# Elementwise sums and products of GpSimd moved to VectorE in a two-block, fp32-accurate network on one core

## The chip, the core and the metric

One core of a Trainium2 chip runs the whole network in one launch. TensorE (PE in the profile) does matmuls into PSUM, VectorE (DVE) and ScalarE (ACT) do elementwise work, GpSimd (POOL) does elementwise work on SBUF alone, and SyncE (SP) issues DMAs. The metric is the device time of one execution in microseconds; the shown time is the median of three runs.

## The reference, cut to what matters

A sequence of 512 tokens of width 1024 goes through two blocks. The first has an even layer (linear recurrent unit and a gated convolution) and an odd one (spatial gating and forgetting attention), each followed by a convolutional gated feed-forward layer. The second, with 256 context tokens beside the 512, has two layers of three branches:

```
h = rms_norm(x, g) * (1 + scale) + shift
aq, ak, av, az, bq, ..., cz, gm = split_proj(h @ w_in)      # a: differential attention, b: mLSTM, c: neighbourhood
...
proj = einsum('btnw,nwd->btnd', stack(ys), w_br)            # three branches
y = sum(sigmoid(gm) * proj, axis=2) @ w_out
x = x + gate * y
```

All inputs and outputs are float32 and the products have to be nearly as exact as that.

## The kernel before, in words

Activations lie with their channels on the 128 partitions and tokens along the free dimension. A matmul operand is held as a high and a low part, both in a form that PE multiplies in one pass (`H` and `L` for the layer's input, `wh` and `wl` for a weight), and each product is three matmuls, high by high, high by low and low by high (`mm3`). A weight is loaded raw (`ws`), ACT copies it to `wh`, DVE subtracts to get `wl` (`wload`). Queries and keys are stacked the same way into halves of 64 rows (`stack`).

The gate projections `gm` of block 2 save matmuls by a scheme of seven half-size products instead of eight. Its left operands are sums of the halves of a pair of weights, which `wpair` forms in place with four 128x512 sums (`ws` and `w2`, on GpSimd; 24 pairs in all). Its right operands are sums of halves of the layer's input, which `halves` forms at the start of each layer: it first adds `H` and `L` back together (eight sums per layer, on GpSimd) and then does four more sums for each group and splits them (DVE and ACT).

Other work that GpSimd has: sums of squares for the norms (`Stream.square`, most of them), a product in `even`, masks on weights and on rows (`odd`, `scan`), products with per-head factors (`mixed`, `head_out`), the rotary sum (`branch_a.prep`), the sum of two directions and one product in `scan`, a product with the norm in `out_proj`, and fills.

The order is not that of the code. `Order` (lines 200 to 440) records every operation with a cost (`_cost`), the tiles it touches and its dependencies, and `flush` then issues them one at a time: on each engine the earliest-recorded operation that can start soonest by the costs, as long as a buffer is free. So each engine runs a fixed list in order, and a change of an operation's engine or cost may reorder all five lists behind it. The costs of the two forms in question are

```
        if eng == "pool":
            return 146 + (2.1 if op == "tensor_tensor" else 3.3) * size
...
        two = not psum and n_in <= 1 and op in ("tensor_copy", "tensor_scalar", "memset")
        return 95 + size / (1.92 if two else 0.96)
```

The planner has no term for two engines that hinder each other. All recorded operations carry one line, 486, in the profile, so groups are told apart by tile names: `s` and `t` are the working buffers of block 2 and block 1, `P` a PSUM bank, `tn` a small one, `C` the constants. A DVE operation that the compiler makes for a reduction with two inputs is named CUSTOM_DVE_ANT_0, or ISA in the order.

Of the kernel before, what the change touches and what calls it, by code (L numbers as in the profile page):

```python
# [9 lines left out]
F32 = mybir.dt.float32  # L10
# [3 lines left out]
ALU = mybir.AluOpType  # L14
# [4 lines left out]
T = 512  # L19
# [491 lines left out]
class Kern:  # L511
# [68 lines left out]
    def wpair(self, srcs):  # L580


        nc = self.nc
        self.n_ += 1
        raw = []
        for i, src in enumerate(srcs):
            st = nc.tile(self.wp, [128, 1088], F32, "wst", self.WST, f"ws{self.n_}_{i}")
            nc.sync.dma_start(out=st[:, :1024], in_=src.rearrange("p k m -> p (k m)"))
            raw.append(st)
        s2 = nc.tile(self.wp, [128, 512], F32, "w2", 1, f"w2{self.n_}")  # L590
        a11, a12, a21, a22 = (raw[i][:, 512 * j:512 * j + 512] for i in range(2) for j in range(2))
        out = {}

        def put(x, names, tags=("whi", "wlo", 1088, 4)):
            self.n_ += 1
            n = 512 * len(names)
            hi = nc.tile(self.wp, [128, tags[2]], F32R, tags[0], tags[3], f"wh{self.n_}")[:, :n]
            lo = nc.tile(self.wp, [128, tags[2]], F32R, tags[1], tags[3], f"wl{self.n_}")[:, :n]
            self.split(hi, lo, x[:, :n])
            for i, a in enumerate(names):  # L600
                out[a] = [y[:, 512 * i:512 * i + 512].rearrange("p (k m) -> p k m", k=4) for y in (hi, lo)]

        sub = lambda o, x, y: nc.gpsimd.tensor_tensor(o, x, y, op=ALU.subtract)
        put(raw[0], ("a11", "a12"))
        sub(a11, a11, a21)
        sub(s2, a22, a11)
        put(s2, ("s2",), ("w2h", "w2l", 512, 1))
        sub(a12, a12, s2)
        put(raw[0], ("s3", "s4"))
        nc.gpsimd.tensor_tensor(a21, a21, a22, op=ALU.add)  # L610
        put(raw[1], ("s1", "a22"))
        return out

# [73 lines left out]
class Stream:  # L687
# [7 lines left out]
    def square(self, x):  # L695
        K, nc = self.K, self.K.nc
        sq = self.new()[:, :self.n]
        nc.scalar.activation(sq, x, AF.Square)
        if self.acc is not None:
            e = nc.vector if self.k in VADD else nc.gpsimd  # L700
            e.tensor_tensor(sq, sq, self.acc, op=ALU.add)
        self.k += 1
        self.acc = sq

# [31 lines left out]
def block1(K, X, out, dbg, mods, B, es):  # L736
# [101 lines left out]
    def even(pre):  # L838
# [29 lines left out]
        for j in range(4):  # L868
            nc.scalar.activation(hh[j], hh[j], AF.Sqrt, scale=0.25)
        for j in range(4):  # L870
            nc.gpsimd.tensor_tensor(ix[j], ix[j], hh[j], op=ALU.mult)
            nc.vector.tensor_tensor_scan(hh[j], aa[j], ix[j], 0.0, ALU.mult, ALU.add)
        for j in range(0, 4, 2):
            for j, p in zip((j, j + 1), scaled(proj(W[4 + j], W[5 + j]), R)):
# [18 lines left out]
    def odd():  # L893
# [23 lines left out]
        wt = [t3(), t3()]  # L917
        for i in range(2):
            nc.sync.dma_start(out=wt[i], in_=A["sgu_wt"][:, 4 * i:4 * i + 4])
            nc.gpsimd.tensor_tensor(wt[i], wt[i], K.c("keep").unsqueeze(1).to_broadcast([128, 4, 128]),  # L920
                                    op=ALU.mult)
        bb = t3()
        nc.sync.dma_start(out=bb, in_=A["sgu_bb"])
# [16 lines left out]
        def mixed():  # L940
# [8 lines left out]
            rg = K.rsqrt(sv, 32)  # L949
            nc.vector.tensor_scalar(sv, rg, 0.5, None, op0=ALU.mult)  # L950
            for n in range(4):
                nc.gpsimd.tensor_tensor(hc(gt[n]), hc(gt[n]),
                                        sv[:, n * 8:(n + 1) * 8].unsqueeze(2).to_broadcast([128, 8, 64]), op=ALU.mult)
            yield
            for j in range(4):
# [18 lines left out]
        def prep(j):  # L974
# [23 lines left out]
            for hp in range(2):  # L998
                st.append(K.stack(q_, k_, hp, t2, T, T))
                h = 2 * j + hp  # L1000
                cb.append(t2())
                nc.sync.dma_start(out=cb[hp], in_=cd[h:h + 1, :].partition_broadcast(128))
                cm.append(t3())
                nc.gpsimd.tensor_tensor(cm[hp], cb[hp].rearrange("p (a b) -> p a b", a=4),
                                        K.c("cmask").unsqueeze(1).to_broadcast([128, 4, 128]), op=ALU.add)
            heads[j] = vt, st, cb, cm
            yield
# [164 lines left out]
SQUARES = 11000.0  # L1172
RATES = 32000.0
COND = 60000.0
VADD = (6, 7)
FIRST = 7

GM = (0, 0, 0, 1, 1, 1, 1, 2, 2, 2, 1, 1)
# [2 lines left out]
class Block2:  # L1181
# [95 lines left out]
    def halves(self, n):  # L1277

        K, nc = self.K, self.nc
        b = self.tk = {q: [] for q in ("b11", "b21", "b22", "t1", "t2", "t3", "t4")}  # L1280
        for k in range(4):
            for nm, r, c in (("b11", k, 0), ("b21", k + 4, 0), ("b22", k + 4, n)):
                b[nm].append((K.H[:, r, c:c + n], K.L[:, r, c:c + n]))
        self.tn = n
        for k in range(4):
            x, y = self.s(2 * n), self.s(2 * n)
            for a, r in ((x, k), (y, k + 4)):
                nc.gpsimd.tensor_tensor(a, K.H[:, r, :2 * n].bitcast(F32), K.L[:, r, :2 * n].bitcast(F32), op=ALU.add)
            b11, b12, b21, b22 = x[:, :n], x[:, n:], y[:, :n], y[:, n:]
            nc.vector.tensor_tensor(b11, b12, b11, op=ALU.subtract)  # L1290
            nc.vector.tensor_tensor(b12, b22, b12, op=ALU.subtract)
            nc.vector.tensor_tensor(b22, b22, b11, op=ALU.subtract)
            nc.vector.tensor_tensor(b21, b21, b22, op=ALU.subtract)
            for a, names in ((x, ("t1", "t3")), (y, ("t4", "t2"))):
                h, l = self.ysplit(a, 2 * n)
                for i, nm in enumerate(names):
                    b[nm].append((h[:, i * n:i * n + n], l[:, i * n:i * n + n]))
            yield
# [94 lines left out]
    def head_out(self, o, ntile, g, gate, c):  # L1393
# [7 lines left out]
        nc.vector.tensor_reduce(ss, b3(sq), axis=AX.X, op=ALU.add)  # L1401
        nc.vector.tensor_scalar(v, ss, 1.0 / 128 / c ** 2, EPS / c ** 2, op0=ALU.mult, op1=ALU.add)
        r = K.rsqrt(v, ntile)
        nc.gpsimd.tensor_tensor(b3(o), b3(o), r.unsqueeze(2).to_broadcast([128, ntile, 128]), op=ALU.mult)
        for q, b, m in self.transposes(o, [i * 128 for i in range(ntile)]):
            d = gate[:, b:b + m]
            nc.vector.scalar_tensor_tensor(d, q, g, d, op0=ALU.mult, op1=ALU.mult)
# [3 lines left out]
    def branch_a(self, lat, ctx, full, out):  # L1411
# [28 lines left out]
        def prep(h):  # L1440
# [4 lines left out]
            for nm, c in (("aq", cq), ("ak", ctx)):  # L1445
# [1 line left out]
                d, w = self.s(), self.s(T)  # L1447
                nc.vector.stream_shuffle(out=w, in_=p[0][0], mask=swap)
                nc.vector.tensor_tensor(d[:, :T], p[0][0], rc, op=ALU.mult)
                nc.gpsimd.tensor_tensor(w, w, rs, op=ALU.mult)  # L1450
                nc.gpsimd.tensor_tensor(d[:, :T], d[:, :T], w, op=ALU.add)
                self.copy(d, p[1:])
                qk.append(d)
                yield
# [133 lines left out]
    def branch_b(self, lat, ctx, full, out):  # L1588
# [31 lines left out]
        def scan(h):  # L1620
# [15 lines left out]
            for d in range(2):  # L1636
# [2 lines left out]
                nc.sync.dma_start(out=b6(m), in_=src.partition_broadcast(128))  # L1639
                nc.vector.tensor_tensor(b6(m), b6(m), cols(self.MIN, d, ntile).to_broadcast([128, ntile, 128]), op=ALU.max)  # L1640
                W = self.s(n)
                nc.gpsimd.tensor_tensor(b6(W), b6(m), K.c("maskf" if d == 0 else "maskb").unsqueeze(1)
                                        .to_broadcast([128, ntile, 128]), op=ALU.add)
                for i in range(ntile):
                    r = slice(i * 128, (i + 1) * 128)
# [5 lines left out]
                    nc.vector.tensor_tensor(W[:, b:b + e], W[:, b:b + e], p, op=ALU.mult)  # L1651

                for b, e in ((0, n),) if not full else ((0, T), (T + 128, n)) if d == 0 else ((0, n - 128),):
                    (nc.vector if d == 0 else nc.gpsimd).tensor_tensor(m[:, b:e], m[:, b:e], q[:, b:e], op=ALU.mult)
                Ws.append(W)
                qa.append(m)
                yield
# [35 lines left out]
            for d in range(2):  # L1693
                for a in range(2):
                    i = slice(a * pb, (a + 1) * pb)
                    nc.vector.tensor_tensor(b6(o[d])[:, i], O[d][a][:, :, :128],
                                            d3(da, d)[:, i].unsqueeze(2).to_broadcast([128, pb, 128]), op=ALU.mult)
            nc.gpsimd.tensor_tensor(o[0], o[0], o[1], op=ALU.add)
            z = self.silu2(self.unit("bz", h, lat, cq))
            yield  # L1700
            t = self.s(n)
# [142 lines left out]
    def out_proj(self, full, out):  # L1844
# [23 lines left out]
        for m in range(8):  # L1868
# [2 lines left out]
            nc.sync.dma_start(out=t[:, :T], in_=self.xd[:, m])  # L1871
            a = (m, w, t, lat, 0, T, S, X, 0)
            if full:
                nc.gpsimd.tensor_tensor(t[:, :T], t[:, :T], R1, op=ALU.mult)
                nc.sync.dma_start(out=t[:, T:], in_=self.A["xc"][:, m])
                if m < 5:
                    some(*a)
# [122 lines left out]
```

## Time and profile before

| | |
|---|---|
| median of 3 runs | 2883.07 us (2879.26 to 2884.18) |
| the profiled execution, its time | 2883.25 us |
| its span | 2881.5 us |
| PE, PEld (weight loads) | 98%, 85% of the span busy |
| DVE, ACT, POOL | 71%, 45%, 14% busy |
| mean granted clock of PE | 0.993 of full speed |
| matmuls | 16280 |

The span is what lies between the first and the last instruction; 1.75 us lie around it. Matmuls overlap: each is shown from its start to its end while the next has already begun, so a busy PE says little, and the waits have to be read from places where PE stood still. Block 1 fills the first 1130 us, the first layer of block 2 the next 990, the second layer the rest.

### The profile page before, as it was taken

The page shows a single profiled execution, that of the slowest core. Times are in us where ns is not written, and L with a number is a line of the kernel's source. Part 1 is how long each engine was busy: PE and PEld are TensorE (multiplying, and loading weights), DVE is VectorE, ACT ScalarE, POOL GpSimd, SP SyncE. Part 2 cuts the span into 40 slices and gives each one's busy share as a digit, 9 for nine tenths or more (in the row PEclk, how much of TensorE's full clock was granted, in tenths as well). Part 3 has the DMA queues.
Part 4 walks back from the last instruction along what each step waited for, and adds up shares of the span by engine and source line. Part 5 has one row for each costly group of instructions (what it writes and reads, how often), then busy time and mean ns, then how long its engine had stood idle before and what let it go on. Part 6 is the DMA issues. An engine that isn't in the chain of part 4 may idle for free. (4 is left out here: it accounts for less than half of the span.)

```text
span 2881.5 us, 42542 instructions
## 1 busy us (share of the span) xinstructions
PE 2831.4 (98%) x16280; PEld 2452.8 (85%) x16280; DVE 2057.3 (71%) x4049; ACT 1306.7 (45%) x2449; POOL 393.4 (14%) x285
## 2 busy tenths in 40 slices
PE   9999999999999999999999999999999999999998
PEld 7888888887888888889899989998878889989887
DVE  7878687478875875855777676575586677787765
ACT  6344234465442443754545453341256554554433
POOL 1010000010100003100211131120210121232201
PEclk9999999999999999999999999999999999999999
DMA  4333433332324423111112132254312222232362
GB/s 171 125 120 124 144 133 110 105 106 80 137 99 145 142 89 118 63 67 57 72 67 71 59 104 92 76 165 164 135 63 94 71 81 71 71 107 96 107 211 92
DMA packets 113245, 302.63 MB, mean 105 GB/s; under 512 B 11657, under 2 KB 25353, under 8 KB 113041
## 3 DMA queue, kind: packets, MB, share of 16 engines
q1 hardware_dynamic: 112896, 299.91, 30.7%
q8 instruction: 128, 2.10, 0.3%
q14 instruction: 77, 0.62, 0.1%
q10 hardware_dynamic: 144, 0.00, 0.0%
HBM read 272.26 MB, written 27.61 MB: 104 GB/s over the span
## 5 line engine op out<-in xcount | busy, mean ns | idle before, releaser
L486 PE MATMUL P<-H,wl 128*128 128x512 f32 (+2 forms) x2648 | 960.9, 363 | 4.0 <-DVE wl L486 4.0
L486 PE MATMUL P<-L,wh 128*128 128x512 f32 (+2 forms) x2648 | 961.2, 363 | 2.5 <-DVE L L486 2.5
L486 PE MATMUL P<-H,wh 128*128 128x512 f32 (+2 forms) x2648 | 960.9, 364 | 1.4 <-ACT H L486 1.4
L486 ACT ACTIVATE wh<-ws 128x1024 fp32r<-128x1024 f32 (+3 forms) x450 | 436.1, 972 | 764.3 <-PE P L486 649.1
L486 DVE TENSOR_TENSOR wl<-ws,wh 128x1024 fp32r<-128x1024 f32 (+3 forms) x450 | 523.3, 1164 | 204.3 <-ACT wh L486 202.4
L486 PEld LDWEIGHTS P<-H,wl 128*128 128x128 f32 x2648 | 500.3, 189 | 82.7 <-DVE wl L486 5.4
L486 PEld LDWEIGHTS P<-L,wh 128*128 128x128 f32 x2648 | 499.6, 189 | 83.3 <-DVE L L486 4.6
L486 PEld LDWEIGHTS P<-H,wh 128*128 128x128 f32 x2648 | 499.0, 188 | 81.4 <-ACT H L486 2.4
L486 PE MATMUL P<-s,wh 128*128 128x256 f32 (+2 forms) x1344 | 330.6, 333 | 0.0
L486 PE MATMUL P<-t,wh 128*128 128x512 f32 x960 | 301.5, 395 | 0.3 <-ACT t L486 0.3
L486 ACT ACTIVATE s<-P 128x512 f32<-128x512 f32 (+3 forms) x416 | 186.6, 482 | 222.9 <-PE P L486 202.7
L486 PE MATMUL P<-s,s 128*128 128x128 f32 (+4 forms) x1576 | 239.1, 293 | 11.9 <-DVE s L486 11.8
L486 PEld LDWEIGHTS P<-s,wh 128*128 128x128 f32 x1344 | 229.6, 189 | 17.6
L486 PEld LDWEIGHTS P<-s,s 128*128 128x128 f32 (+1 forms) x1576 | 212.8, 192 | 28.7 <-issue 10.2
L486 PE MATMUL P<-s,wl 128*128 128x256 f32 (+2 forms) x672 | 222.8, 332 | 2.1 <-DVE wl L486 2.1
L486 PEld LDWEIGHTS P<-t,wh 128*128 128x128 f32 x960 | 180.4, 188 | 43.0 <-ACT t L486 0.6
L486 ACT ACTIVATE s<-s 128x768 f32<-128x768 f32 (+7 forms) x226 | 153.3, 694 | 114.7 <-DVE s L486 97.9
L486 DVE TENSOR_TENSOR s<-s,s 128x512 f32<-128x512 f32 (+8 forms) x200 | 173.9, 875 | 26.2 <-ACT s L486 11.9
L486 PE MATMUL P<-t,wl 128*128 128x512 f32 x480 | 189.8, 395 | 0.0
L486 POOL TENSOR_TENSOR s<-s,s 128x512 f32<-128x512 f32 (+2 forms) x76 | 102.8, 1356 | 582.2 <-DVE s L486 317.7
L486 ACT ACTIVATE s<-P,tn 128x512 f32<-128x512 f32 (+1 forms) x224 | 117.8, 534 | 107.0 <-DVE tn L486 106.9
L486 ACT ACTIVATE t<-t 128x512 f32<-128x512 f32 (+4 forms) x162 | 97.5, 611 | 123.5 <-DVE t L486 122.6
(145 smaller groups left out, 3579.8 us busy)
## 6 DMA issues: line engine op xcount, KB each, us to landing
ws<-in_w2in SPq DMA_DIRECT2D x136, 512.0 KB, 3.3
ws<-in_up SPq DMA_DIRECT2D x88, 512.0 KB, 3.2
wm<-in_w_mod SPq DMA_DIRECT2D x48, 512.0 KB, 4.4
ws<-in_down SPq DMA_DIRECT2D x32, 384.0 KB, 3.1
ws<-in_w2br SPq DMA_DIRECT2D x48, 256.0 KB, 2.7
ws<-in_down SPq DMA_DIRECT2D x32, 320.0 KB, 2.9
ws<-in_w0in SPq DMA_DIRECT2D x18, 512.0 KB, 3.7
gd<-s SPq DMA_DIRECT2D x24, 384.0 KB, 2.9
```

What stands on the lines that cost most here:

```text
L486: o["f"](*o["a"], **o["k"])
```

## The change

Every sum and product that was on GpSimd is put on VectorE, 273 operations; GpSimd keeps its 12 fills. In `square` the list of steps that were already on DVE (`VADD`) goes. Nothing else is edited, but the planner now prices these operations as DVE's and orders all engines anew.

```diff
@@ wpair
-        sub = lambda o, x, y: nc.gpsimd.tensor_tensor(o, x, y, op=ALU.subtract)
+        sub = lambda o, x, y: nc.vector.tensor_tensor(o, x, y, op=ALU.subtract)
...
-        nc.gpsimd.tensor_tensor(a21, a21, a22, op=ALU.add)
+        nc.vector.tensor_tensor(a21, a21, a22, op=ALU.add)
@@ Stream.square
-            e = nc.vector if self.k in VADD else nc.gpsimd
-            e.tensor_tensor(sq, sq, self.acc, op=ALU.add)
+            nc.vector.tensor_tensor(sq, sq, self.acc, op=ALU.add)
@@ halves
-                nc.gpsimd.tensor_tensor(a, K.H[:, r, :2 * n].bitcast(F32), K.L[:, r, :2 * n].bitcast(F32), op=ALU.add)
+                nc.vector.tensor_tensor(a, K.H[:, r, :2 * n].bitcast(F32), K.L[:, r, :2 * n].bitcast(F32), op=ALU.add)
@@ head_out
-        nc.gpsimd.tensor_tensor(b3(o), b3(o), r.unsqueeze(2).to_broadcast([128, ntile, 128]), op=ALU.mult)
+        nc.vector.tensor_tensor(b3(o), b3(o), r.unsqueeze(2).to_broadcast([128, ntile, 128]), op=ALU.mult)
@@ branch_a.prep
-                nc.gpsimd.tensor_tensor(w, w, rs, op=ALU.mult)
-                nc.gpsimd.tensor_tensor(d[:, :T], d[:, :T], w, op=ALU.add)
+                nc.vector.tensor_tensor(w, w, rs, op=ALU.mult)
+                nc.vector.tensor_tensor(d[:, :T], d[:, :T], w, op=ALU.add)
...
```

The same exchange of `gpsimd` for `vector` is made in `even`, `odd`, `mixed`, `branch_b.scan` (mask, product, sum) and `out_proj`.

What it does to the order is shown at three places. The first is DVE's list at the start of block 2, where `halves` begins (`s_9695`, `s_9696`, `s_9732` are the first of its sums; `s_9672` is the first subtraction of a `stack` that PE needs next; `wl` are weights):

```order
 L486 SCALAR_TENSOR_TENSOR L<-t_2040,mod_79,H 128x512
+L486 TENSOR_TENSOR s_9695<-H,L 128x768
 L486 TENSOR_TENSOR wl_2064<-ws_2062,wh_2063 128x1024
 L486 TENSOR_TENSOR wl_2067<-ws_2065,wh_2066 128x1024
-L486 TENSOR_TENSOR wl_9799<-ws_9797,wh_9798 128x1024
+L486 TENSOR_TENSOR s_9696<-H,L 128x768
 L486 TENSOR_TENSOR s_9695<-s_9695 128x384
 L486 TENSOR_TENSOR s_9695<-s_9696,s_9695 128x384
+L486 TENSOR_TENSOR s_9696<-s_9696,s_9695 128x384
+L486 TENSOR_TENSOR s_9732<-H,L 128x768
 L486 TENSOR_TENSOR s_9672<-s_9667,s_9672 64x768
```

Three of the eight sums now stand on DVE ahead of the stack, with one more step of 128x384, and a weight's low part has gone behind it.

The second is DVE's list at the first weight pair of layer 0, inside the neighbourhood attention (`s_9973` and `s_9976` are rows of probabilities that PE transposes next, `ws_0_10056`, `ws_1_10057` and `w_10058` the pair and its sums):

```order
 L486 TENSOR_SCALAR s_9961<-s_9961,tn_9956 128x512
 L486 TENSOR_TENSOR tn_9971<-tn_9969 128x2
+L486 TENSOR_TENSOR ws_0_10056<-ws_0_10056,ws_1_10057 128x512
 L486 RECIPROCAL tn_9971<-tn_9971 128x2
+L486 TENSOR_TENSOR ws_1_10057<-ws_1_10057 128x512
 L486 TENSOR_SCALAR s_9973<-s_9973,tn_9971 128x512
 L486 TENSOR_SCALAR s_9976<-s_9976,tn_9971 128x512
+L486 TENSOR_TENSOR w_10058<-ws_1_10057,ws_0_10056 128x512
+L486 TENSOR_TENSOR ws_0_10056<-ws_0_10056,w_10058 128x512
+L486 TENSOR_TENSOR wl_10062<-w_10058,wh_10061 128x512
```

Two of the pair's four sums stand ahead of the second two rows, two behind them.

The third is PE's list in layer 1 where a head's output (`s_12235`, scaled by GpSimd before, by DVE now) is transposed into `P_12334`, between matmuls of the gates of branch b:

```order
 L486 MATMUL P_12383<-wh_12378,H 128x272
-L486 MATMUL P_12334<-C,s_12235 128x128 x4
 L486 MATMUL P_12383<-wh_12378,L 128x272
 L486 MATMUL P_12383<-wl_12379,H 128x272
@@ -12411,4 +12409,5 @@
 L486 MATMUL P_12384<-wh_12378,H 128x272
 L486 MATMUL P_12384<-wh_12378,L 128x272
+L486 MATMUL P_12334<-C,s_12235 128x128 x4
```

The transposes have gone behind 22 more matmuls.

## Rows read from the trace of the kernel before

**Rows 1.** The page, part 1: busy time, share of the span, instructions of each engine.

```profile
PE 2831.4 (98%) x16280; PEld 2452.8 (85%) x16280; DVE 2057.3 (71%) x4049; ACT 1306.7 (45%) x2449; POOL 393.4 (14%) x285
```

**Rows 2.** Timeline at 8 us: start, length, engine, line, operation, tiles, shapes, count.

```profile
8.15 0.40 PE L486 MATMUL P<-L,wh 128*128 128x512 f32 x1
8.15 0.19 PEld L486 LDWEIGHTS P<-H,wl 128*128 128x128 f32 x1
8.39 0.39 PE L486 MATMUL P<-H,wl 128*128 128x512 f32 x1
```

**Rows 3.** What PE waited for, whole span: us in total, times, longest.

```profile
PE P L486 <- DVE s L486: 21.2, 20, 4.1
PE P L486 <- DVE wl L486: 6.8, 7, 1.9
PE P L486 <- DVE t L486: 3.7, 3, 1.5
...
PE P L486 <- POOL s L486: 2.0, 2, 1.2
```

**Rows 4.** Groups by shape: count, busy us, mean ns of one, idle before.

```profile
L486 POOL TENSOR_TENSOR s<-s,s 128x512 f32<-128x512 f32 x53 | 73.6, 1389 | 388.7 <-DVE s L486 243.3 <-PE P L486 69.6 <-ACT s L486 62.2
L486 POOL TENSOR_TENSOR s<-H,L 128x768 f32<-128x768 f32 x8 | 18.1, 2294 | 34.1 <-DVE L L486 34.1
L486 DVE TENSOR_TENSOR t<-t,t 128x512 f32<-128x512 f32 x64 | 44.1, 689 | 2.5 <-ACT t L486 1.5
L486 DVE TENSOR_TENSOR s<-s,s 128x512 f32<-128x512 f32 x42 | 36.6, 874 | 2.3 <-DMA s<-cmd 2.0
L486 DVE TENSOR_TENSOR s<-s,s 128x768 fp32r<-128x768 f32 x20 | 18.9, 953 | 0.6 <-issue 0.5
```

**Rows 5.** Timeline of layer 0's `halves`, 1142 to 1172 us; GpSimd, DVE, PE.

```profile
1142.09 18.09 POOL L486 TENSOR_TENSOR s<-H,L 128x768 f32<-128x768 f32 x8 [34.13 <-DVE L L486]
...
1151.32 2.91 DVE L486 TENSOR_TENSOR wl<-ws,wh 128x1024 fp32r<-128x1024 f32 x1 [1.72 <-ACT wh L486]
...
1154.15 2.21 DVE L486 TENSOR_TENSOR s<-s 128x384 f32<-128x384 f32 x1
...
1156.47 5.51 DVE L486 TENSOR_TENSOR s<-s,s 128x384 f32<-128x384 f32 x3
...
1162.71 0.55 PE L486 MATMUL P<-s,s 128*128 128x256 f32 x1 [4.07 <-DVE s L486]
...
1171.47 0.55 DVE L486 TENSOR_TENSOR s<-s 128x384 f32<-128x384 f32 x1
```

**Rows 6.** What PE waited for, layer 1's `halves`, 2118 to 2156 us.

```profile
PE P L486 <- DVE s L486: 3.0, 1, 3.0
PE P L486 <- DVE L L486: 2.2, 2, 1.5
```

**Rows 7.** Timeline at a weight pair, 1273 to 1279 us, and one row without GpSimd.

```profile
1174.41 0.88 DVE L486 TENSOR_SCALAR s<-s,tn 128x512 f32<-128x512 f32 x2
...
1273.96 1.41 POOL L486 TENSOR_TENSOR ws<-ws,ws 128x512 f32<-128x512 f32 x1 [113.78 <-DVE wl L486]
...
1277.05 2.65 DVE L486 TENSOR_SCALAR s<-s,tn 128x512 f32<-128x512 f32 x2
...
1278.44 0.63 PE L486 MATMUL P<-C,s 128*128 128x128 f32 x4 [1.78 <-DVE s L486]
```

**Rows 8.** Timeline at a head's output in layer 1.

```profile
2479.58 1.04 POOL L486 TENSOR_TENSOR s<-s,tn 128x512 f32<-128x512 f32 x1 [8.11 <-issue]
...
2480.68 0.55 PE L486 MATMUL P<-C,s 128*128 128x128 f32 x3 [0.81 <-POOL s L486]
```

**Rows 9.** Stretches: length, PE busy (count), granted clock, DMA share, GB/s.

```profile
1161.00:1168.00 7.00, 5.29 (x25) 0.51 0.00 0
...
2154.30:2157.80 3.50, 3.50 (x18) 0.51 0.02 5
```

**Rows 10.** A slice of layer 1, all engines: length, busy (count) each, clock, DMA.

```profile
2521.00:2593.00 72.00, 68.00 (x443) 61.53 (x442) 57.53 (x138) 37.62 (x81) 22.20 (x17) 0.95 0.32 105
```

More of the change, by code (lines that the diff above doesn't have):

```diff
@@ L870, in even @@
         for j in range(4):
-            nc.gpsimd.tensor_tensor(ix[j], ix[j], hh[j], op=ALU.mult)
+            nc.vector.tensor_tensor(ix[j], ix[j], hh[j], op=ALU.mult)
             nc.vector.tensor_tensor_scan(hh[j], aa[j], ix[j], 0.0, ALU.mult, ALU.add)
@@ L919, in odd @@
             nc.sync.dma_start(out=wt[i], in_=A["sgu_wt"][:, 4 * i:4 * i + 4])
-            nc.gpsimd.tensor_tensor(wt[i], wt[i], K.c("keep").unsqueeze(1).to_broadcast([128, 4, 128]),
+            nc.vector.tensor_tensor(wt[i], wt[i], K.c("keep").unsqueeze(1).to_broadcast([128, 4, 128]),
                                     op=ALU.mult)
@@ L951, in mixed @@
             for n in range(4):
-                nc.gpsimd.tensor_tensor(hc(gt[n]), hc(gt[n]),
+                nc.vector.tensor_tensor(hc(gt[n]), hc(gt[n]),
                                         sv[:, n * 8:(n + 1) * 8].unsqueeze(2).to_broadcast([128, 8, 64]), op=ALU.mult)
@@ L1003, in prep @@
                 cm.append(t3())
-                nc.gpsimd.tensor_tensor(cm[hp], cb[hp].rearrange("p (a b) -> p a b", a=4),
+                nc.vector.tensor_tensor(cm[hp], cb[hp].rearrange("p (a b) -> p a b", a=4),
                                         K.c("cmask").unsqueeze(1).to_broadcast([128, 4, 128]), op=ALU.add)
@@ L1174 @@
 COND = 60000.0
-VADD = (6, 7)
 FIRST = 7
@@ L1641, in scan @@
                 W = self.s(n)
-                nc.gpsimd.tensor_tensor(b6(W), b6(m), K.c("maskf" if d == 0 else "maskb").unsqueeze(1)
+                nc.vector.tensor_tensor(b6(W), b6(m), K.c("maskf" if d == 0 else "maskb").unsqueeze(1)
                                         .to_broadcast([128, ntile, 128]), op=ALU.add)
@@ L1653, in scan @@
                 for b, e in ((0, n),) if not full else ((0, T), (T + 128, n)) if d == 0 else ((0, n - 128),):
-                    (nc.vector if d == 0 else nc.gpsimd).tensor_tensor(m[:, b:e], m[:, b:e], q[:, b:e], op=ALU.mult)
+                    nc.vector.tensor_tensor(m[:, b:e], m[:, b:e], q[:, b:e], op=ALU.mult)
                 Ws.append(W)
@@ L1697, in scan @@
                                             d3(da, d)[:, i].unsqueeze(2).to_broadcast([128, pb, 128]), op=ALU.mult)
-            nc.gpsimd.tensor_tensor(o[0], o[0], o[1], op=ALU.add)
+            nc.vector.tensor_tensor(o[0], o[0], o[1], op=ALU.add)
             z = self.silu2(self.unit("bz", h, lat, cq))
@@ L1873, in out_proj @@
             if full:
-                nc.gpsimd.tensor_tensor(t[:, :T], t[:, :T], R1, op=ALU.mult)
+                nc.vector.tensor_tensor(t[:, :T], t[:, :T], R1, op=ALU.mult)
                 nc.sync.dma_start(out=t[:, T:], in_=self.A["xc"][:, m])
```

## The prediction, made before the changed kernel was run

> **What bounds the kernel now.** First the page's engine line: PE is busy for 2831.4 of 2881.5 us, DVE for 71%, GpSimd for 14% [rows 1]. That alone would say that 50 us can be gained at most and that GpSimd matters little. So next the pace of PE in a stretch where nothing is missing: matmuls of 512 columns start 0.24 us apart although each is shown for 0.40 us, with a weight load of 0.19 us for each [rows 2]. A wait therefore shows as idle time only beyond the 0.16 us by which two matmuls overlap; the idle time is a floor of what is lost, and a good one for waits of a microsecond. Since the number of matmuls doesn't change, the time after is the time before, less the waits that go, plus the waits that come.
>
> The page on reading traces (the Trainium skill, Perfetto Trace Analysis, Identifying the Most-Contended Engine) says that matmul busy time is no good measure of headroom, and that the share of weight loads is one. By that page the 85% of the weight loads would leave 15%, some 430 us as an estimate. The rows disagree: at full pace a load of 0.19 us per 0.24 us is 79% [rows 2], so 85% is a full engine, and the sum below doesn't use it.
>
> Then what PE waited for. DVE leads: 21.2 us in 20 waits for an `s` tile, 6.8 us for low parts of weights, 3.7 us for `t` tiles; directly for GpSimd there are only 2.0 us in two waits [rows 3]. Few, long waits, and almost none of them names GpSimd. The question is what made DVE late there.
>
> **What the change adds and removes on the engines.** GpSimd did 273 sums and products: 221 of 128x512, 28 of 128x768, 4 of 128x640 and 20 of 128x256 by the code's shapes. One of 512 takes it 1.389 us, one of 768 up to 2.294 us; DVE does them in 0.689 and 0.953 us where nothing disturbs it [rows 4]. On DVE they cost 221 x 0.689 + 28 x 0.953 = 179 us, and the 24 small ones some 12 us by the same slope (0.26 us per 256 columns less), 191 us in all, over a span of 2881 us. So DVE's busy share would go from 71% to 78% if nothing else happened.
>
> Something else happens. The same DVE form, sum of two `s` tiles of 512, means 0.874 us in block 2 against 0.689 us for `t` tiles in block 1 [rows 4], and the long ones lie beside GpSimd's. At the start of layer 0, GpSimd works for 18.09 us without a break; in that stretch DVE needs 2.21 us for one step of 128x384, which takes 0.55 us later when GpSimd is still [rows 5]. At the first weight pair two row scalings take DVE 2.65 us beside GpSimd and 0.88 us without it [rows 7]. So a DVE operation that meets a GpSimd one is held for about the rest of it. What that costs DVE in total lies between 42 x 0.185 = 8 us (the one form of [rows 4]) and all of GpSimd's 393 us [rows 1]; since most DVE groups in the trace show no excess I take about 100 us, nearer the lower end. DVE's load after is then about 2057 + 191 - 100 = 2150 us, 75%. None of this is in the time directly, because PE bounds it. It sets how late DVE is at the few places where PE waits for it.
>
> **The places, worked out by hand.** *Layer 0's `halves`.* From 1151.32 us DVE does a weight's low part (2.91), one step of 128x384 (2.21), and a group of three, the last two of which are the stack that PE needs (5.51), together with small gaps 10.7 us; the two casts follow, and PE stands for 4.07 us [rows 5]. In the new order the low part has gone behind, and DVE has in that place two sums of 768 (0.953 each [rows 4]), three steps of 128x384 (0.55 each [rows 5]) and two subtractions of 64x768 (0.95 each, as long as any of 768): 5.5 us. That is 5.2 us earlier, more than the wait of 4.07 us. What is late next is ACT, which makes the high parts of the stack in the same microseconds; I count 4 us saved, with 2 us as the other end.
>
> *Layer 1's `halves`.* The same mechanism with 512 columns: PE waits 3.0 us for a stack and 2.2 us for low parts of the input that stood behind held steps of DVE [rows 6]. Eight sums of 0.689 us come onto DVE's list, 5.5 us, but only two of them stand ahead of the last low parts. I count 3.5 of the 5.2 us saved, and between 1.5 and 5.2.
>
> *Weight pairs.* At the first pair both pairs of row scalings are held, and PE waits 1.78 us for them and 0.78 us for what follows. Without GpSimd the second pair ends at 1273.74 (where the first pair began) + 0.88 + 2 x 0.69 for the two sums now ahead + 0.88 and some 0.2 of small steps, that is 1277.1, where it ended at 1277.05 + 2.65 = 1279.7 [rows 4, 7]. The wait ended 2.6 us earlier is all of it. There are six such places with a wait of PE just behind a pair's sums, 0.7 to 2.6 us each and 7.9 us together; I count 6 us, since two sums of four stand ahead each time and eat a part where the wait was short, and between 3 and 7.9.
>
> *Half-clock stretches.* After such waits PE runs at a granted clock of 0.51, which is the lower of its two levels: 7 us from 1161 us on, 3.5 us from 2154.3 us on [rows 9]. A stretch costs half its length. Five of them (6.8, 3.4, 3.4, 3.4 and 3.4 us) follow the waits above or the similar ones at 1695 to 1707 us; all gone would give back 10 us. I count 3.5, the one at 1161 us, and between 0 and 10.
>
> *What is lost.* A product that GpSimd did in 1.04 us while DVE went on with its own list now stands in that list. The clearest is the scaled head output at 2479.58 us, for which PE waited 0.81 us [rows 8]. DVE reaches it some 2.5 us later, behind four reductions; but the planner has put 22 more matmuls (22 x 0.12 us, 2.7 us) ahead of the transposes, so this costs nothing and gains nothing. That cover is what the whole loss hangs on: where no matmul could be put ahead, a product of 0.69 us and its queue become a wait. Block 1's order is nearly unchanged on PE (some 400 of 5300 matmuls in other places) and its DVE list grows by 53 sums, most of them squares that nobody awaits. I count 2 us lost, between 0 and 12.
>
> Sum: -4 - 3.5 - 6 - 3.5 + 2 = -15 us. Made against the profiled execution, 2883.25 us, which is the median of the runs within 0.2 us: **2868 us**. With all terms at their good ends it is 2883 - 27 = 2856, with all at their bad ones 2883 - 6.5 + 12 = 2889.
>
> **The rivals.** *The waits only move.* The order of block 2 changes in hundreds of rows, and a fixed order made by costs that know nothing of PE's real lateness leaves waits wherever it is a little wrong. For it: the waits of [rows 3] are few and their places look accidental. Against it: the long ones sit beside GpSimd, which the planner has no price for, and that cause is removed, not moved. If three quarters of the gain come back elsewhere, 2883 - 17 + 13 = 2879 us, no change that can be told.
>
> *DVE becomes the bound (slower).* Place: the dense slices of block 2, as at 2521 us, where DVE is busy for 57.5 of 72 us and GpSimd for 22.2 us in 15 operations [rows 10]. These add 15 x 0.69 = 10 us to DVE, 68 of 72. It decides from the point where DVE is not shortened by what it is held today, so that it goes from 71% to 78% of the whole span. Waits behind an engine in a queue grow about as one over its free share: 31.7 us of waits for DVE [rows 3] times 0.29 / 0.22 is 42, so 10 us more, and with none of the gains the time is 2893 us. The held operations of [rows 5, 7] speak against it. The page's rule on the two engines (the Trainium skill, Perfetto Trace Analysis, Optimizing Scalar/DVE Operations) is the same rival: when DVE is saturated, work may be moved to GpSimd, the opposite of this change, with the caution that the two share a read port and that it may not help. DVE is at 71% on the mean and at 80% in such a slice, so here the rule's condition is near but not met.
>
> *Everything goes well.* All of the waits named go, the clock stays up, and the shorter chains help at small waits too: 2852 us.
>
> *The change doesn't do what it says*, in that DVE's long operations had another cause: then only the 2.0 us of direct waits can go and the load comes on top, which is the slower case.
>
> **How the numbers follow.** A measurement of this kernel can tell about 0.2%, 6 us, from no change. Forecast, 2868 (own range 2857 to 2877): 0.64. Everything goes well: 0.07. The waits only move: 0.16. DVE the bound, with the last rival: 0.13. Faster by over 0.2% is the first and second, 0.71; same is the third, 0.16; slower is the fourth, 0.13. The range reaches from 2852 to 2889, which takes in the third case and the bad ends of the terms and leaves out most of the slower case and half of the very good one.
>
> **What would show it.** In the profile after, GpSimd is down to fills, DVE is busy for 2100 to 2180 us, and the sum of two `s` tiles of 512 means 0.69 us instead of 0.87; if it stays at 0.87 the cause was another. PE's waits for `s` tiles fall from 21.2 to about 10 us, the wait of 4.07 us at the start of layer 0 is gone, and so is the half clock there. The forecast is wrong if DVE's busy time grows by 190 us, or if PE's waits for DVE in the slices after 2300 us grow by as much as those at the starts of the layers shrink.

## The result, and the profile of the changed kernel

The changed kernel takes **2849.64 us** (median of four runs, 2848.51 to 2850.61) where the kernel before takes 2881.99 us beside it: ratio 0.9888, 95% interval 0.9871 to 0.9905. That is 32 us less, more than twice the 15 us of the forecast and 2.4 us below the low end of its range. The direction was the forecast one; the size wasn't, and only a part of the gain came in the way that was forecast.

The engine line of the page after, to be put beside [rows 1]:

```profile
span 2847.9 us, 42206 instructions
PE 2822.3 (99%) x16280; PEld 2447.0 (86%) x16280; DVE 2117.3 (74%) x4322; ACT 1307.6 (46%) x2449; POOL 1.1 (0%) x12
```

DVE took over 273 operations that cost it 191 us by the durations of [rows 4], and its busy time rose by 60.0 us. So the operations that it had before became 131 us shorter in all (the prediction took 100 us). PE's idle time is the span less its busy time: 50.1 us before, 25.6 us after.

The groups by shape (count, busy us, mean ns of one, idle before) that answer to [rows 4]:

```profile
L486 DVE TENSOR_TENSOR s<-s,s 128x512 f32<-128x512 f32 x95 | 68.6, 727 | 7.0 <-ACT s L486 6.1 <-DMA s<-xd 0.2
L486 DVE TENSOR_TENSOR s<-H,L 128x768 f32<-128x768 f32 x8 | 7.5, 951 | 0.1
```

The sums of `H` and `L` that took GpSimd 2294 ns take DVE 951, and the sum of two `s` tiles fell from 874 to 727 ns, not to the 690 that were forecast. The trace shows why: eight of the 42 such sums of before read their first input as 64 by 8 elements instead of 512 in a row, and they take 1174 ns before and 1183 after, with GpSimd at work or not. The other 34 took 804 ns on the mean; after, they and the moved ones take 685. So of the 8 us that the prediction read off this row as held by GpSimd [rows 4], half was never held.

What PE waited for over the whole span (us, times, longest), to be put beside [rows 3]:

```profile
PE P L486 <- DVE s L486: 8.5, 10, 2.6
PE P L486 <- ACT s L486: 5.4, 6, 2.9
...
PE P L486 <- DVE t L486: 1.4, 1, 1.4
PE P L486 <- DVE wl L486: 0.3, 1, 0.3
```

Now by place. The view of stretches gives length, busy us (count) of PE, PEld, DVE, ACT and POOL, granted clock, DMA share and GB/s; length less PE's busy time is PE's idle time. Before:

```profile
560.00:740.00 180.00, 175.91 (x1110) 147.56 (x1109) 141.51 (x376) 101.43 (x203) 25.51 (x17) 1.00 0.29 102
...
1120.00:1225.00 105.00, 97.40 (x634) 85.44 (x633) 87.34 (x193) 63.19 (x137) 18.09 (x8) 0.97 0.19 66
1225.00:1655.00 430.00, 422.84 (x2887) 390.87 (x2886) 283.81 (x656) 217.86 (x520) 59.24 (x44) 1.00 0.18 65
1655.00:1725.00 70.00, 65.99 (x379) 61.24 (x379) 57.20 (x129) 35.43 (x78) 26.07 (x18) 0.95 0.36 112
...
2080.00:2170.00 90.00, 84.81 (x510) 73.13 (x509) 71.97 (x161) 46.72 (x92) 17.42 (x12) 0.98 0.21 73
2170.00:2520.00 350.00, 346.63 (x2442) 312.43 (x2441) 249.18 (x559) 190.16 (x444) 58.78 (x43) 1.00 0.22 77
2520.00:2600.00 80.00, 76.00 (x487) 68.40 (x486) 63.86 (x154) 41.18 (x87) 24.54 (x19) 0.96 0.31 103
2600.00:2815.00 215.00, 213.03 (x1299) 188.54 (x1299) 154.06 (x301) 84.89 (x145) 37.85 (x30) 1.00 0.43 143
```

After, the same pieces of the program, with bounds moved by the time saved ahead of them:

```profile
560.00:740.00 180.00, 179.72 (x1132) 151.62 (x1131) 147.24 (x397) 102.19 (x206) 0.00 (x0) 1.00 0.32 108
...
1120.00:1215.00 95.00, 89.39 (x578) 76.86 (x577) 79.85 (x191) 61.01 (x127) 0.00 (x0) 0.98 0.18 63
1215.00:1640.00 425.00, 425.00 (x2911) 393.42 (x2910) 301.10 (x712) 219.41 (x532) 0.22 (x2) 1.00 0.19 67
1640.00:1705.00 65.00, 64.02 (x392) 59.31 (x391) 56.29 (x132) 36.14 (x78) 0.00 (x0) 1.00 0.38 113
...
2055.00:2145.00 90.00, 89.98 (x553) 77.94 (x553) 73.99 (x178) 52.09 (x102) 0.00 (x0) 1.00 0.21 72
2145.00:2495.00 350.00, 347.80 (x2461) 314.61 (x2457) 261.12 (x608) 188.84 (x446) 0.00 (x0) 1.00 0.23 79
2495.00:2575.00 80.00, 76.35 (x473) 68.44 (x472) 65.16 (x167) 39.52 (x79) 0.22 (x2) 0.94 0.29 97
2575.00:2785.00 210.00, 209.46 (x1269) 185.26 (x1268) 159.50 (x326) 85.59 (x145) 0.22 (x2) 1.00 0.45 148
```

Read the idle time down the two lists: 4.1, 7.6, 7.2, 4.0, 5.2, 3.4, 4.0 and 2.0 us before; 0.3, 5.6, 0.0, 1.0, 0.0, 2.2, 3.7 and 0.5 us after. No stretch rose. In the 425 us of layer 0 that hold the weight pairs PE doesn't stand still at all.

The other part is the clock. These are the stretches of before at the lower level, beside [rows 9] (same columns):

```profile
1280.50:1283.90 3.40, 3.40 (x34) 3.07 (x30) 1.35 (x6) 2.05 (x9) 0.00 (x0) 0.51 0.02 5
1697.00:1700.40 3.40, 3.40 (x13) 3.40 (x14) 3.02 (x5) 0.85 (x1) 3.28 (x2) 0.50 0.30 116
1707.20:1710.60 3.40, 3.40 (x15) 3.40 (x14) 3.05 (x5) 3.40 (x12) 0.93 (x1) 0.50 0.15 41
2570.80:2577.60 6.80, 5.85 (x26) 5.68 (x27) 5.00 (x11) 5.59 (x10) 3.09 (x3) 0.50 0.11 40
2871.20:2881.50 10.30, 2.24 (x8) 1.86 (x8) 3.81 (x12) 0.83 (x3) 0.00 (x0) 0.50 0.46 155
```

And those of after:

```profile
1163.00:1166.40 3.40, 3.40 (x12) 2.61 (x11) 3.22 (x15) 3.40 (x16) 0.00 (x0) 0.50 0.01 2
2538.60:2548.80 10.20, 9.16 (x38) 8.27 (x39) 8.22 (x18) 5.84 (x14) 0.00 (x0) 0.50 0.14 52
2838.90:2847.90 9.00, 1.76 (x8) 1.38 (x7) 3.38 (x11) 0.26 (x1) 0.00 (x0) 0.50 0.42 147
```

Inside the program 27 us at the lower level became 13.6 us, and half of the difference, some 7 us, came back (the stretch at the program's end stayed). Idle time (-24.5) and clock (-7) make -31.5 of the span's -33.6 us. So almost nothing of the gain was hidden in short waits: here idle time and clock were no mere floor but nearly the whole.

### The profile page after: what moved, and what is told of

Same layout as the page of the kernel before. It is cut to its first block, busy times and chain, and to the rows that moved or that the text cites. A ratio compares the mean times of both kernels' runs of the same rounds, so it can differ in the third digit from the quotient of the medians.

```text
span 2847.9 us, 42206 instructions
## 1 busy us (share of the span) xinstructions
PE 2822.3 (99%) x16280; PEld 2447.0 (86%) x16280; DVE 2117.3 (74%) x4322; ACT 1307.6 (46%) x2449; POOL 1.1 (0%) x12
## 4 chain that ended last, share of the span: by engine, by line
PE 95%; ACT 2%; DVE 2%; issue 0%; DMA 0%; DVEq 0%; SPq 0%; ACTq 0%
PE P L486 94%; DVE s L486 1%; ACT s L486 1%; PE P L488 1%; ACT wh L486 0%; DMA X<-in_x 0%; DVE wl L486 0%; ACT t L486 0%; DMA V<-in_vec 0%; DVE t L486 0%; ACT H L486 0%; DVE tn L486 0%; ACT L486 0%; DVE L L486 0%; ACT tn L486 0%
## 5 line engine op out<-in xcount | busy, mean ns | idle before, releaser
L486 DVE TENSOR_TENSOR wl<-ws,wh 128x1024 fp32r<-128x1024 f32 (+3 forms) x450 | 499.9, 1112 | 176.6 <-ACT wh L486 170.0
L486 DVE TENSOR_TENSOR s<-s,s 128x512 f32<-128x512 f32 (+7 forms) x276 | 205.7, 753 | 30.9 <-ACT s L486 24.3
L486 ACT ACTIVATE s<-s 128x512 f32<-128x512 f32 (+7 forms) x226 | 153.5, 695 | 98.5 <-DVE s L486 95.8
L486 DVE SCALAR_TENSOR_TENSOR t<-t,V,t 128x511 f32<-128x511 f32 (+1 forms) x196 | 145.3, 745 | 3.1 <-ACT t L486 1.6
```

What stands on the lines that cost most here:

```text
L486: o["f"](*o["a"], **o["k"])
```

## The experiments

The kernel before ran beside each group; its medians were 2881.6 to 2882.7 us. Theory 1 is the prediction's: GpSimd holds DVE's operations. The rivals are theory 2, that the new order made the gain, and theory 3, that the chains got shorter because DVE is faster at a sum than GpSimd.

**The hindrance by itself.** In the two next kernels the order of after stays as it is. Behind each moved operation GpSimd works on a spare bfloat16 tile of zeros, released by a fill of one column on DVE:

```diff
+        nc.vector.tensor_tensor(*a, **k)
+        nc.vector.memset(D[:, 512 + i:513 + i], 0.0)
+        w = D[:, i + 1:i + 513]
+        nc.gpsimd.tensor_tensor(w, w, w, op=ALU.mult)
```

> The kernel after in its own order, and behind each of the 273 moved operations GpSimd does a product of 128x512 of a spare tile of zeros that nobody reads; a fill of one column on DVE releases it (273 x some 0.06 us, 16 us of DVE). Theory 1 (GpSimd's operations that read hold DVE's): DVE's busy time rises by 60 to 140 us beyond the 16, and the time returns to 2865 to 2885 us though nobody waits for GpSimd. Theory 3 (the gain came from the shorter chain and DVE's faster operation, not from the hindrance): 2850 to 2856 us.

In the second kernel the last line is a fill:

```diff
-        nc.gpsimd.tensor_tensor(w, w, w, op=ALU.mult)
+        nc.gpsimd.memset(w, 0.0)
```

> As the run with spare products, but GpSimd fills the same spare tile instead of multiplying it, so that it writes and reads nothing. If a GpSimd operation holds DVE only where both read: 2850 to 2856 us, DVE's sum of two `s` tiles of 512 at 0.73 us or less. If any work of GpSimd holds DVE: as slow as the run with spare products.

With the products 2894.55 us (ratio to before 1.0040, 1.0025 to 1.0055); with the fills 2849.59 us (0.9886, 0.9870 to 0.9903), the time of after. The engine lines, products first, then fills:

```profile
PE 2833.4 (98%) x16280; PEld 2450.1 (85%) x16280; DVE 2232.1 (77%) x4595; ACT 1308.2 (45%) x2449; POOL 351.3 (12%) x286
```

```profile
PE 2819.6 (99%) x16280; PEld 2443.6 (86%) x16280; DVE 2123.0 (75%) x4595; ACT 1307.8 (46%) x2449; POOL 148.8 (5%) x286
```

PE, ACT and DVE never wait for GpSimd in either. The products make DVE's same instructions 109 us longer and the kernel 45 us slower. The groups by shape say which are held (a mean takes in those that met no product or fill). Products:

```profile
L502 DVE TENSOR_TENSOR wl<-w,wh 128x512 fp32r<-128x512 f32 x24 | 30.1, 1254 | 0.0
L502 DVE TENSOR_SCALAR s<-s,tn 128x512 f32<-128x512 f32 x64 | 32.1, 543 | 0.6
L502 DVE TENSOR_TENSOR t<-P,t 128x512 f32<-128x512 f32 x112 | 77.0, 689 | 65.8 <-PE P L502 62.1 <-ACT t L502 3.5
```

Fills:

```profile
L502 DVE TENSOR_TENSOR wl<-w,wh 128x512 fp32r<-128x512 f32 x24 | 16.5, 688 | 1.0 <-ACT wh L502 1.0
L502 DVE TENSOR_SCALAR s<-s,tn 128x512 f32<-128x512 f32 x64 | 28.9, 493 | 0.6
L502 DVE TENSOR_TENSOR t<-P,t 128x512 f32<-128x512 f32 x112 | 77.1, 690 | 71.6 <-PE P L502 67.9 <-ACT t L502 3.5
```

The low part of a pair's sum, which follows a moved operation at once and has both inputs in SBUF, goes from 688 to 1254 ns beside a product. Of the 112 sums with one input in PSUM only four met a product, and these took 676 to 692 ns; 23 such sums of 256 columns met one and took 416 ns, as the others did. So GpSimd's products hold DVE, and theory 3 is not enough by itself: DVE does the 273 sums itself in this kernel, and the gain is gone all the same. What share of the real gain the shorter chains have isn't shown: in the kernel before ACT waited 51.5 us for tiles that GpSimd made, and the change takes GpSimd out of these chains together with the holding. Two limits: the fills keep GpSimd busy for 149 us and the products for 351, so fills were tried for a shorter time; and 40 of the 109 us fall on three operations of the pairs, two of which, sums, were not on DVE in the kernel before.

The page on the memory (the Trainium skill, SBUF — State Buffer, Who interferes with whom) says just this: a DVE instruction with two inputs from SBUF competes with a GpSimd instruction that reads SBUF, not with one that only writes, one with at most one such input does not compete outside the modes that use two ports, and the one that comes second is blocked until the first has finished. The rows agree where they touch it: in the kernel with products a low part that met a running product ended some 0.55 us after that product's end, most often 1.5 us after its own start, and the five that had begun ahead of the next product took 674 to 683 ns.

**Engine and order apart.** The change does two things: another engine does the work, and the planner, which knows that, orders everything anew. First the engine without the order:

```diff
-        self.gpsimd = _Engine(self, "pool", nc.gpsimd)
+        self.gpsimd = _Engine(self, "pool", nc.gpsimd); self.moved = _Engine(self, "pool", nc.vector)
...
-        sub = lambda o, x, y: nc.gpsimd.tensor_tensor(o, x, y, op=ALU.subtract)
+        sub = lambda o, x, y: nc.moved.tensor_tensor(o, x, y, op=ALU.subtract)
...
```

> The 273 sums and products run on DVE, but are planned with GpSimd's prices on a list of their own, so the order of PE, ACT and SP is that of the kernel before and DVE's list is the old one with the 273 put in. Theory 1 (GpSimd held DVE's operations): most of the gain of 32 us comes without any new order, 2850 to 2860 us, DVE busy near 2117 us, PE's waits for `s` below 12 us. Theory 2 (the new order made the gain): 2875 to 2895 us, since the load is added to DVE and the order is the old one.

And the order without the engine, with `_Engine(self, "dve", nc.gpsimd)` in that place:

> The order of the kernel after on PE, ACT and SP, but the 273 operations run on GpSimd (planned as DVE's, issued to GpSimd). Theory 1 (GpSimd held DVE's operations): no gain is left, 2875 to 2900 us, the sum of two `s` tiles of 512 on DVE again means over 0.85 us. Theory 2 (the new order made the gain): 2850 to 2862 us.

In place: 2871.83 us (0.9963, 0.9950 to 0.9976). Order alone: 2869.39 us (0.9955, 0.9940 to 0.9970). All four expectations missed: engine and order give about a third each, -11 and -13 us, and together -33 us, more than their sum. Neither theory alone explains the gain. The engine lines, in place first:

```profile
PE 2826.3 (99%) x16280; PEld 2445.4 (85%) x16280; DVE 2118.1 (74%) x4322; ACT 1308.5 (46%) x2449; POOL 1.1 (0%) x12
```

```profile
PE 2829.5 (99%) x16280; PEld 2449.6 (85%) x16280; DVE 2054.1 (72%) x4049; ACT 1308.8 (46%) x2449; POOL 390.3 (14%) x285
```

In place, DVE is as little held as in after (2118.1 us), but 191 us of work stand where the planner took DVE for free, and PE still waits for `s` tiles:

```profile
PE P L486 <- DVE s L486: 21.8, 27, 2.6
```

With the order alone, DVE is held as in before: 2054.1 us for what takes 2117.3 - 191 = 1926 us unhindered, so 128 us of holding. In one and the same order, that of after, GpSimd as the engine therefore costs 2869.4 - 2849.6 = 20 us; that is its holding together with its slower sums, which these runs don't part. In the order of before, the engine is worth 11 us, net of the load that the order didn't plan for.

PE's list is that of before in the first kernel and that of after in the second, so each can be cut at the same matmuls as its model. Two pieces of each, block 1's and layer 0's scan head, in place first:

```profile
560.00:740.00 180.00, 176.44 (x1109) 147.07 (x1109) 143.83 (x392) 100.84 (x203) 0.00 (x0) 1.00 0.31 103
1645.00:1714.00 69.00, 64.99 (x380) 59.19 (x379) 58.97 (x144) 35.45 (x76) 0.00 (x0) 0.98 0.35 114
```

```profile
560.00:740.00 180.00, 179.14 (x1144) 151.00 (x1143) 137.78 (x374) 103.69 (x208) 22.54 (x17) 1.00 0.31 100
1651.00:1720.00 69.00, 65.98 (x390) 60.56 (x390) 53.07 (x118) 35.92 (x78) 23.34 (x15) 0.98 0.33 106
```

| idle time of PE, us | before | in place | order alone | after |
|---|---|---|---|---|
| block 1, 560 to 740 us of before | 4.1 | 3.6 | 0.9 | 0.3 |
| layer 0's `halves` | 7.6 | 7.6 | 8.0 | 5.6 |
| layer 0's pairs | 7.2 | 1.7 | 0.8 | 0.0 |
| layer 0's scan head | 4.0 | 4.0 | 3.0 | 1.0 |
| layer 1's `halves` | 5.2 | 2.6 | 3.0 | 0.0 |

Block 1's wait goes with the new order, though GpSimd works as before, and stays when only the engine changes. The pairs' waits go with either. Layer 0's `halves` and its scan head need both.

**Parts.** Halves alone, pairs alone, the rest alone (each the lines of the diff ahead that belong to it, the others left on GpSimd), and halves with pairs:

> The kernel before with the 16 sums of `halves` alone on DVE. By the prediction's terms (two places and one half-clock stretch, 4 + 3.5 + 3.5 us): 2870 to 2873 us, with the waits at the starts of both layers of block 2 gone. If waits only move between places: 2878 to 2884 us.

> The kernel before with the 96 sums of the 24 weight pairs alone on DVE. By the prediction's term (six places): 2874 to 2878 us. If the pairs' sums hold DVE at many places where the wait is too short to be seen as idle PE: 2862 to 2872 us, with DVE's busy time up by less than half of the 66 us that they cost it.

> The kernel after with the sums of `halves` and of the weight pairs (112 of the 273) given back to GpSimd, so 161 operations moved. The prediction counted nothing for these places but a loss of 2 us: 2882 to 2886 us. If they carry what the prediction missed (33 us less the parts of the two runs beside it): 2862 to 2872 us.

> The kernel before with the sums of `halves` and of the weight pairs (112 operations) on DVE, the other 161 on GpSimd. If the parts add (10 + 18 us): 2851 to 2856 us, and the other 161 are worth 2 to 6 us. If they overlap, because one frees DVE also for the other: 2858 to 2864 us, and the 161 are worth 9 to 14 us. If the 161 only cost: 2842 to 2849 us, a kernel better than both.

| on DVE | us | ratio to before (95%) | gain |
|---|---|---|---|
| halves, 16 sums | 2871.95 | 0.9962 (0.9947 to 0.9977) | 9.9 |
| pairs, 96 sums | 2863.75 | 0.9934 (0.9917 to 0.9950) | 18.1 |
| the other 161 | 2879.13 | 0.9990 (0.9981 to 1.0000) | 2.7 |
| halves and pairs | 2855.02 | 0.9911 (0.9894 to 0.9927) | 26.9 |

The parts add: 9.9 + 18.1 = 28.0 against 26.9 together, and 30.7 with the rest against 32.4. Each part has an order of its own, though, and orders scatter by as much (below), so a fit this close is partly luck. The 161 met neither expectation and can't be told from no change. Halves came out close to the prediction (11 counted with their clock stretch). The pairs are worth three times the 6 us counted. Their page and two stretches:

```profile
PE 2824.1 (99%) x16280; PEld 2447.7 (86%) x16280; DVE 2062.6 (72%) x4145; ACT 1307.3 (46%) x2449; POOL 259.9 (9%) x189
```

```profile
1225.00:1655.00 430.00, 429.99 (x2947) 398.78 (x2946) 294.31 (x699) 224.08 (x532) 26.67 (x22) 1.00 0.20 69
1655.00:1720.00 65.00, 63.14 (x381) 58.92 (x379) 49.37 (x122) 30.61 (x69) 13.84 (x8) 0.97 0.35 100
```

The 96 sums are 66 us more work for DVE, and its busy time rose by 5.3 us: what it was held by them (61 us) is nearly what they cost it. All 7.2 us of idle time of layer 0's middle go with them, in an order made for them, and half of the 4.0 us at the scan head behind it, where the prediction had counted nothing.

The pairs were taken apart into engine and order as well, with the same two lines as above for the pairs' sums only:

> The pairs' 96 sums alone, run on DVE but planned as GpSimd's: the order of the kernel before on PE, ACT and SP, with the sums put into DVE's list where GpSimd would have had them. The pairs with their own order gained 18 us (2863.8 us). If the gain is that DVE is no longer held: 2862 to 2870 us, no wait of PE over 0.5 us left between 1225 and 1655 us. If it is the new order: 2876 to 2884 us.

> The pairs' 96 sums planned as DVE's but run on GpSimd: the order of the run with the pairs alone, with GpSimd still at work beside DVE. If the gain is that DVE is no longer held: 2876 to 2886 us. If it is the new order: 2862 to 2870 us. A time between, as both whole-kernel runs gave, would say that each gives a part.

In place 2866.06 us (0.9945, 0.9928 to 0.9961), order alone 2874.55 us (0.9975, 0.9966 to 0.9984). Most of the pairs' gain, 15.5 of 18 us, comes with no new order, and since PE's list is then that of before, no other draw of an order can explain it. In place, two waits of up to 1.1 us are left between 1225 and 1655 us, so not quite all:

```profile
PE P L486 <- DVE s L486: 1.4, 2, 1.1
```

**How much is the draw of an order.** Why an order made for DVE should gain 13 us while GpSimd still holds it was not explained. One guess was that a planner that takes DVE for busier puts more matmuls ahead of it. So the price of a DVE operation was raised in the kernel before, and then, towards what the trace shows, in the kernel after:

```diff
-        return 95 + size / (1.92 if two else 0.96)
+        return 152 + size / (1.92 if two else 0.96)
```

> The kernel before, all operations on their old engines, with the planner's fixed price of a DVE operation raised by 57 ns to 152, near what the trace shows (0.689 us for 512 columns instead of 0.628). It asks why the new order alone, with GpSimd still at work, gained 13 us. Theory 4 (the order got better because the planner took DVE for busier and put more matmuls ahead of what DVE makes): 2862 to 2876 us. Theory 5 (the gain comes from the places of the moved operations themselves): 2880 to 2886 us.

> The kernel after with the planner's fixed price of a DVE operation at 152 ns instead of 95, near what the trace shows for 512 columns (0.689 us). With no operation held any more the price is true for each: if true prices help the order, 2838 to 2846 us, fewer short waits; if the order is as good as it gets at these sizes, 2847 to 2856 us.

> As the run with DVE's price at 152 ns, and PE's price of a matmul raised by 8% (512 columns: 233 ns instead of 216; the trace shows starts 240 ns apart), so that the ratio of the two engines is again near the old one. If the ratio matters and not the prices: 2847 to 2853 us; if both true prices help: 2836 to 2845 us.

> The kernel after with only PE's price of a matmul raised by 8%, DVE's left at 95 ns. If the two price effects add (2872 with DVE's, 2860 with both): 2835 to 2843 us, the best so far. If a price change of this size draws another order without a direction: 2847 to 2872 us.

On the kernel before it did nothing: 2883.32 us (1.0002, 0.9993 to 1.0011). The guess fell. On the kernel after, each "truer" price made it slower: DVE's 2872.16 us (0.9968, 0.9956 to 0.9980), PE's 2865.54 us (0.9941, 0.9925 to 0.9958), both 2860.50 us (0.9926, 0.9911 to 0.9941). None of the three met an expectation of a better order, and they have no direction: both together lose less than DVE's or PE's alone. Therefore the price was changed by next to nothing on both kernels, to 97 and to 91:

> The kernel before with the planner's fixed price of a DVE operation at 97 ns instead of 95. Theory 6 (the new order's gain belongs to the change): 2877 to 2887 us. Theory 7 (orders scatter): anywhere from 2868 to 2892 us, over 5 us away from 2882 in one of the two kernels of before.

> The kernel before with that price at 91 ns. Theory 6: 2877 to 2887 us. Theory 7: over 5 us away from 2882 in one of the two kernels of before.

> The kernel after with that price at 97 ns. Theory 6: 2846 to 2855 us. Theory 7: 2850 is a good draw, and one of the two kernels of after lies at 2857 us or above.

> The kernel after with that price at 91 ns. Theory 6: 2846 to 2855 us. Theory 7: one of the two kernels of after lies at 2857 us or above.

| price of a DVE operation | before, us | after, us | difference |
|---|---|---|---|
| 91 | 2891.67 | 2853.24 | 38.4 |
| 95 (as it is) | 2881.99 | 2849.64 | 32.4 |
| 97 | 2877.60 | 2848.35 | 29.3 |
| 152 | 2883.32 | 2872.16 | 11.2 |

Both theories were partly right. Orders scatter: a price changed by 4 ns, which means nothing, moves the kernel before by 10 us (1.0033, 1.0022 to 1.0045). But the kernel after is the faster at every price, and its small changes scatter less (2848 to 2853 us). At one price in both kernels the change is worth 11 to 38 us; the 32 us measured are one such pair. Of the 13 us of the order alone a part can be a draw of this kind, and these runs can't say how much. The kernel at 97 on DVE's price (0.9881, 0.9865 to 0.9898) can't be told from after (0.9888).

## Why the prediction was right in direction and short in size

Its steps in its own order, idle time of PE from the stretches shown above:

| term of the sum | forecast (bounds), us | measured, us |
|---|---|---|
| layer 0's `halves` | -4 (-2 to -4) | -2.0 |
| layer 1's `halves` | -3.5 (-1.5 to -5.2) | -5.2 |
| weight pairs | -6 (-3 to -7.9) | -9.8 (7.2, 1.2 and 1.4 in three stretches) |
| half-clock stretches | -3.5 (0 to -10) | -7 |
| lost in DVE's queue | +2 (0 to +12) | 0; no stretch rose |
| scan heads | 0 | -3.4 (3.0 and 0.4) |
| block 1 | 0 | -4.0 |
| sum | -15 | -31.4 of a span shorter by 33.6 |

- *What bounds the kernel*: right. PE's waits were what there was to gain, and hardly any of them named GpSimd.
- *DVE's load*: right in its sum. 2117 us, where 2100 to 2180 were given; PE's waits for `s` fell to 8.5 us, where about 10 were. One of its readings was not: half the excess of the 874 ns belongs to eight sums that are as long without GpSimd.
- *Layer 0's `halves`*: right that PE's wait for DVE would go and that ACT would be late next; wrong in what ACT would be late with. The wait of 4.07 us for DVE [rows 5] became one of 2.93 us for ACT. It wasn't the high parts of the stack: ACT waited for one of the sums of `halves`, now late in DVE's list, cast it, loaded a table, and only then read the bank that PE wanted. ACT and PE after:

```profile
1159.04 0.84 ACT L486 ACTIVATE s<-s 128x768 fp32r<-128x768 f32 x1 [2.23 <-DVE s L486]
1159.90 1.28 ACT L486 ACT_TABLE_LOAD   x1
1161.20 0.47 ACT L486 ACTIVATE s<-P,tn 128x256 f32<-128x256 f32 x1
```

```profile
1161.82 0.50 PE L486 MATMUL P<-H,wh 128*128 128x512 f32 x1 [2.93 <-ACT s L486]
```

So the gain is at the small end that was given, that it came by ACT is partly luck, and half of the clock stretch stayed.

- *The first weight pair*: right in its arithmetic. The second two rows were to end 3.3 us after the first began; they end 3.06 us after:

```profile
1265.93 0.88 DVE L486 TENSOR_SCALAR s<-s,tn 128x512 f32<-128x512 f32 x2
...
1266.79 0.68 DVE L486 TENSOR_TENSOR ws<-ws,ws 128x512 f32<-128x512 f32 x1
...
1267.51 0.69 DVE L486 TENSOR_TENSOR ws<-ws 128x512 f32<-128x512 f32 x1
1268.12 0.87 DVE L486 TENSOR_SCALAR s<-s,tn 128x512 f32<-128x512 f32 x2
```

- **The step that failed** is twofold. First, the pairs' term was too small: it took six waits that stand just behind a pair's sums, 7.9 us, and cut them to 6. The pairs alone gained 18.1 us, and 15.5 us with PE's order unchanged. The 18.1 us are 12.4 us of idle time (50.1 less 37.7) and some 5 us of clock (27 us at the lower level inside the program before, 17 us with the pairs moved). DVE's lateness reached further than the wait just behind. Second, the new order was put down as a loss alone, +2 us with 0 to 12 as its bounds. With GpSimd still at work it gained 13 us, at layer 0's pairs above all (7.2 us of idle time became 0.8) and in block 1's stretch from 560 us on (4.1 became 0.9, while 3.6 stayed in place, so the relief of DVE isn't what ended that wait). How much of the 13 us another draw of the order would give stays open. Layer 0's scan head, left at zero, belongs to both: 4.0 us in place, 3.0 with the order alone, 1.0 after.
- *The clock term* was inside its bounds, at twice the value taken, and not for its reason: of the stretch that it counted, the one at 1161 us, half stayed. Four others went (1280, 1697, 1707 and 2154 us), two of them behind waits at zero in the sum, and the one at 2571 us grew from 6.8 to 10.2 us.
- *The loss* doesn't show in after: no stretch rose. In place it does, where the order has no room for the moved sums: layer 0's stretch behind the scan head, without idle time before, has 1.7 us of it.
- *The range* had for its low end the terms' good ends; for the places left at zero it allowed the 4 us between 2856 and 2852, and they brought 7 us. It was missed by 2.4 us, less than a price changed by 4 ns moves the time: at 91 the kernel after takes 2853.24 us. So the miss of the range is partly luck; the size of the pairs' term and the gain of the order are not in the sum at any draw.
- *The rivals.* That waits only move: one did, from DVE to ACT. That DVE becomes the bound: not here. Its 2893 us, for DVE at 78% without relief, lie near the 2894.55 us of the kernel with spare products, which has DVE at 77%; but that DVE is held and not loaded, and no run measured how waits grow with the load, so this is no test of it. The scan head of layer 1 stayed (4.0 and 3.7 us of idle time) though GpSimd was busy beside it for 24.5 of 80 us before; why is not shown.

## What to carry to other kernels

An engine that PE hardly ever waits for can still set the time, by holding another engine's operations: look for operations of one form that take twice as long at some times, and ask of each what ran beside it, since a mean also holds what is slow by itself. Count the relief over every place that the held engine feeds, not only behind the nearest one. Moving work onto the busier engine paid here, where a third of the time that GpSimd worked (128 of 390 us) had been taken from DVE. And where a planner orders the program, run the new engine in the old order and the new order on the old engine, and test the scatter with a price changed by nothing, before a gain of 10 us is explained.

## What the runs showed of the hardware

In the kernel with spare products, 22 of the 24 low parts of a pair's sum met a product on GpSimd. Those that came while it ran took 0.99 to 1.56 us, those that came first 0.67 to 0.68; beside fills all took 0.68 to 0.69. The scaling of rows by one number per row has a single input tile and is held too: five of 64 met a product and took 1.26 us, the other 59 took 0.48; beside fills two of five took 0.83, the other three 0.48. Sums with one input from PSUM took the same beside a product as without one (416 ns for 256 columns, 23 and 77 of them).

128 us of holding cost 20 us in the order of after with the sums on GpSimd, and 109 us cost 45 us when DVE had the sums as well. The two differ in DVE's load (2054 and 2232 us busy) and in which operations are held, and no run parts these.
